# State-space batches of a two-layer encoder: the skip term as small TensorE products, five fixed PSUM banks, and separate buffers for outputs and in-chunk kernel

## The chip, the cores and the metric

The kernel runs on one core of a Trainium2 chip. A core has five engines that run side by side, each with its own in-order instruction queue: PE (TensorE, matrix products into PSUM), DVE (VectorE), ACT (ScalarE), POOL (GpSimd) and SP (SyncE, which here only issues DMAs). ACT issues a few DMAs as well. PSUM, where products land, has eight banks; each holds 128 partitions of 512 float32. The metric is the device time of one execution in microseconds; the median of several runs is compared.

## The reference

Input `x` is 1024 frames of 1024 channels in float32. Layer 0 projects the normalised input once; the projection feeds a state-space branch and a retention branch, each multiplied by its own SiLU gate, and one output projection follows. Layer 1 is a convolution module. Each layer adds to a residual, and a last RMS norm ends the work. Only the state-space branch matters here. In the reference, for each of 64 groups of 16 channels with 64 complex states:

```python
        bu_re = jnp.einsum('tbgh,gnh->tbgn', u_c, bb_re)
        bu_im = jnp.einsum('tbgh,gnh->tbgn', u_c, bb_im)
        pr, pim, zr, zi = lax.associative_scan(
            _complex_affine_combine, (a_r, a_i, bu_re, bu_im), axis=0)
        xr = zr + pr * s_re - pim * s_im
        xi = zi + pr * s_im + pim * s_re
        y = (jnp.einsum('tbgn,ghn->tbgh', xr, cre)
             - jnp.einsum('tbgn,ghn->tbgh', xi, cim)
             + dsk * u_c)
```

The term `dsk * u_c` is the skip: each channel's input times one number of that channel.

## The kernel before, in words

The front of layer 0 (`layer0_front`) makes the combined projection in blocks of 128 output columns. Blocks `u0` to `u7` are the inputs of the state-space branch; blocks `g8` to `g23` are the sixteen gate blocks. Each block is 2 halves of 512 frames times 8 row blocks times 3 products (float32 kept as a high and a low part: `xh`,`xl` and `wh`,`wl`), so 48 products of 512 columns on PE. DVE evacuates each half (line 393, times the norm factor R), ACT applies SiLU (394). The weight of a block is loaded by SP, its high part made on ACT (189) and its low part on DVE (190), two blocks ahead, in three rotating buffers.

Between the gate blocks lie eight state-space batches B = 0..7 of eight groups each. Time is cut into steps of 8 frames; within such a step a short convolution kernel acts, across steps a scan over 128 steps. A batch goes through four pieces:

- `s5_tables(B)`, one pair of gate blocks ahead: POOL makes the tables Mr, Mi, Tc, Ts and W3 (lines 766 to 768, 18 instructions); ACT makes R8 (839, four instructions, named R in the trace); for B > 1 DVE makes W2r and W2i from small tables that SP loads (806 to 811).
- `s5_states(B)`, traced at the start of gate block g(2B+8): PE makes V = W2 times U into two banks (868, 32 products); DVE turns V by Tc and Ts, scans it (883) and turns it back into S (876 to 895). PE makes the in-chunk kernel `kp` (902, 903), ACT copies columns 16 to 127 of it into `Kg` (905), and DVE writes columns 0 to 15 of `Kg` as the sum of `kp` and the skip table `dd` (906). PE transposes `Kg` into a second bank `kt` (908), ACT copies that (910), SP writes it to memory (912) and reads it back eightfold shifted as `Wd` (915), and ACT reorders `Wd` into W1 (917; the trace names W1 and W3 both W). `Wd` lies in the buffer of tag "yb".
- `s5_out(B)`, traced after gate block g(2B+10), one batch later: PE makes the output y from W1 and U (932) and from W3 and S (938) in two banks, ACT copies both into `yb` (942), which has the same single buffer as `Wd`, and stores it (944).

All these banks come from a pool of five (`ps_aux`) that hands out any free one; the gate blocks use three other banks. The order of the instructions on each engine is not written out by hand: a planner at build time simulates the program and puts every engine's instructions in an order by priority (the order in which they were traced, unless `at` sets it) and by its simulated time of readiness. `issue_after(x)` adds the rule that an instruction comes behind x on x's engine. On the chip every engine then follows that order, and waits in place for whatever is late. `retention` follows the front; it takes its banks from the same `ps_aux`.

## Time and profile before

| what | value |
|---|---|
| median of 3 runs | 1142.81 us (1140.18 to 1144.8) |
| the profiled execution | 1149.41 us, span 1147.6 us |
| mean granted PE clock | 0.993 |
| PE busy | 1125.1 us (98%) |
| DVE busy | 850.0 us (74%) |
| POOL busy | 654.7 us (57%) |
| ACT busy | 489.0 us (43%) |
| gate blocks and state-space batches | about 97 to 323 us of the span |

The profiled execution took 6.6 us longer than the median of the runs. Products on PE overlap, so a busy PE need not be at its peak; what counts is whether it waited, and at which clock it ran. A row of the timeline gives start, duration, engine, line, operation, the tiles as output<-inputs, shape and count, and in square brackets the engine's idle time before it with what ended it. A row of the waits gives the waiting instruction, what released it, the total, how often, and the longest. A row of the windows gives, for a stretch of the span, each engine's busy time and number of instructions, then the granted PE clock, the DMA share and GB/s.

### The profile page before, as it was taken

Reading aid. Unit: us, or ns where it says so; the run is one execution under the profiler, and the core shown is the slowest. Engines: PE = TensorE matmul, PEld = TensorE weight load, DVE = VectorE, ACT = ScalarE, POOL = GpSimd, SP = SyncE. Lnnn points to the kernel's source line nnn. Section 1 sums busy time; section 2 is a strip of 40 time slices with the busy share of each in tenths; the row PEclk is TensorE's granted clock in tenths of the full one; section 3 lists DMA queues with packets and bytes.
Section 4 is the critical chain, followed back from the end, with each engine's and each line's share of the span. In section 5 each row is a group of like instructions: output and inputs, shape, how many; then the busy total and the mean of one; then the engine's idle time right before and its main releaser. Section 6 shows DMA issues by size and latency. Waiting matters only on the chain.

```text
span 1147.6 us, 17204 instructions
## 1 busy us (share of the span) xinstructions
PE 1125.1 (98%) x6286; PEld 984.8 (86%) x6286; DVE 850.0 (74%) x1464; ACT 489.0 (43%) x719; POOL 654.7 (57%) x448
## 2 busy tenths in 40 slices
PE   9999989999999999999999999999999999999897
PEld 7888878888888888989887888888888888888787
DVE  6975778887417569486669522599999899999844
ACT  6423222232223231323436423545545676444673
POOL 2059999998236355232575111589544568677563
PEclk9999999999999999999999999999999999999999
DMA  9344345555378766859998988665778655367865
GB/s 353 110 135 153 120 151 175 194 186 179 133 259 278 265 215 193 284 185 333 386 361 299 318 297 283 189 234 203 250 246 297 239 178 172 121 195 250 273 229 191
DMA packets 117636, 261.45 MB, mean 228 GB/s; under 512 B 10672, under 2 KB 42288, under 8 KB 116912
## 3 DMA queue, kind: packets, MB, share of 16 engines
q1 hardware_dynamic: 114096, 247.78, 64.2%
q10 hardware_dynamic: 3456, 12.58, 2.9%
q8 instruction: 49, 0.80, 0.3%
q14 instruction: 35, 0.29, 0.1%
HBM read 181.48 MB, written 74.65 MB: 223 GB/s over the span
## 4 chain that ended last, share of the span: by engine, by line
PE 36%; DVE 8%; DMA 5%; POOL 2%; issue 2%; ACT 1%; POOLq 0%; SPq 0%; DVEq 0%; ACTq 0%
DVE cv L1534 6%; PE mm_wo L201 5%; PE mm_wo L200 5%; PE mm_wo L202 5%; PE mm_b L201 2%; PE mm_b L202 2%; PE mm_b L200 2%; PE mm_a L202 2%; PE mm_a L201 2%; PE mm_a L200 2%; PE mm_oc L202 2%; PE mm_oc L201 1%; PE mm_oc L200 1%; DMA yn<-yn_d 1%; DMA yg<-gs_d 1%
## 5 line engine op out<-in xcount | busy, mean ns | idle before, releaser
L1534 DVE SCALAR_TENSOR_TENSOR cv<-u,convw,cv 128x512 f32<-128x512 f32 x398 | 273.0, 749 | 6.7 <-ACT cv L1513 4.8
L1507 POOL TENSOR_TENSOR tp<-tp,tp 128x512 f32<-128x512 f32 x64 | 83.0, 1298 | 34.2 <-ACT tp L1506 33.2
L200 PE MATMUL mm_g<-xh,wh_g 128*128 128x512 f32 x256 | 99.6, 389 | 0.0
L201 PE MATMUL mm_g<-xl,wh_g 128*128 128x512 f32 x256 | 97.8, 382 | 0.0
L202 PE MATMUL mm_g<-xh,wl_g 128*128 128x512 f32 x256 | 97.7, 382 | 0.0
L437 POOL TENSOR_TENSOR s1q<-s1q,s1q 128x512 f32<-128x512 f32 x12 | 17.6, 1467 | 81.3 <-ACT s1q L432 81.3
L1506 ACT ACTIVATE tp<-u,convw 128x512 f32<-128x512 f32 x64 | 45.4, 718 | 36.1 <-POOL tp L1507 35.3
L200 PEld LDWEIGHTS mm_g<-xh,wh_g 128*128 128x128 f32 x256 | 48.9, 191 | 8.7 <-issue 1.2
L202 PEld LDWEIGHTS mm_g<-xh,wl_g 128*128 128x128 f32 x256 | 48.7, 190 | 7.1
L201 PEld LDWEIGHTS mm_g<-xl,wh_g 128*128 128x128 f32 x256 | 48.8, 191 | 6.9 <-issue 0.4
L190 POOL TENSOR_TENSOR wl_glu<-wf_glu,wh_glu 128x1024 fp32r<-128x1024 f32 x14 | 34.0, 2428 | 30.9 <-ACT wh_glu L189 30.9
L201 PE MATMUL mm_oc<-zl,wh_woc 128*128 128x512 f32 (+1 forms) x144 | 51.6, 359 | 0.0
L200 PE MATMUL mm_oc<-zh,wh_woc 128*128 128x512 f32 (+1 forms) x144 | 51.6, 370 | 0.0
L202 PE MATMUL mm_oc<-zh,wl_woc 128*128 128x512 f32 (+1 forms) x144 | 51.3, 359 | 0.2 <-DMA wl_woc<-lo_woc 0.2
L190 POOL TENSOR_TENSOR wl_v<-wf_v,wh_v 128x1024 fp32r<-128x1024 f32 x12 | 30.7, 2559 | 35.2 <-ACT wh_v L189 35.2
L393 DVE TENSOR_TENSOR gt<-mm_g,R 128x512 f32<-128x512 f32 x32 | 21.8, 682 | 38.6 <-PE mm_g L202 38.6
L201 PE MATMUL mm_u<-xl,wh_u 128*128 128x512 f32 x128 | 48.4, 381 | 0.7 <-DVE xl L316 0.7
L200 PE MATMUL mm_wo<-ysh,wh_wos 128*128 128x512 f32 x128 | 48.9, 382 | 0.0
L200 PE MATMUL mm_g<-h1h,wh_cg 128*128 128x512 f32 x128 | 48.9, 382 | 0.0
L201 PE MATMUL mm_b<-h1l,wh_cb 128*128 128x512 f32 x128 | 48.7, 381 | 0.1
L202 PE MATMUL mm_b<-h1h,wl_cb 128*128 128x512 f32 x128 | 48.6, 380 | 0.0
L201 PE MATMUL mm_wo<-ysl,wh_wos 128*128 128x512 f32 x128 | 48.5, 379 | 0.0
(526 smaller groups left out, 3641.5 us busy)
## 6 DMA issues: line engine op xcount, KB each, us to landing
wf_g<-w_ab SPq DMA_DIRECT2D x16, 512.0 KB
wf_wos<-w_out SPq DMA_DIRECT2D x16, 512.0 KB
wf_wor<-w_out SPq DMA_DIRECT2D x16, 512.0 KB
wf_cb<-w_c SPq DMA_DIRECT2D x16, 512.0 KB
wf_ca<-w_c SPq DMA_DIRECT2D x16, 512.0 KB
wf_woc<-w_out_c SPq DMA_DIRECT2D x16, 512.0 KB
wf_v<-w_v SPq DMA_DIRECT2D x12, 512.0 KB
wf_cg<-w_c SPq DMA_DIRECT2D x11, 512.0 KB
```

The source lines that it names most:

```text
L190: self.low_made = lo[i].tensor_tensor(wl[:].rearrange(fl)[:, c], wf[:, c], h.bitcast(F32), op=ALU.subtract)
L200: nc.tensor.matmul(ps, wh[:, kb, :], xh, start=start, stop=False, **more)
L201: nc.tensor.matmul(ps, wh[:, kb, :], xl, start=False, stop=False, **more)
L202: self.last_mm = nc.tensor.matmul(ps, wl[:, kb, :], xh, start=False, stop=stop, **more)
L393: nc.vector.tensor_tensor(nat(gt[:, c]), un(ps[:]), nat(self.R[:, c]), op=ALU.mult)
L437: nc.gpsimd.tensor_tensor(a, a, sq[:], op=ALU.add)
L1506: nc.scalar.mul(sk[:], u[:, k:k + HALF], cw[:, nb, k:k + 1])
L1507: gp.tensor_tensor(s0[:], s0[:], sk[:], op=ALU.add)
L1534: v.scalar_tensor_tensor(dst[:], *tap, accs_[i][:], op0=ALU.mult, op1=ALU.add)
```

## The change

1. The skip moves from DVE to PE. Between the two kinds of `kp` products PE now adds, per quarter, a product of a 32-column slice of the identity with the 16 columns of `dd`, into columns 0 to 15 of `kp`. The DVE sum is gone; `Kg` is one ACT copy of all 128 columns.
2. The banks of the batches are fixed: five tags y0, y1, v0, v1, kp with one bank each (`ps_s5`). `kt` is the second quarter of bank kp. The W2 of the first two batches, made by transposes, uses y0 and y1. The work before the batches and the retention each have a pool of five of their own.
3. `Wd` has a buffer of its own (4 KB a partition), no longer that of `yb`. The scratch that the program keeps for DMA descriptors is cut to 1024 bytes.
4. The W1 copy becomes `s5_local(B)`, traced after `s5_out(B-1)`, and comes behind the last `yb` copy of batch B-1 on ACT.
5. Two gates on DVE: the last two instructions of W2 (810, 811) come behind the evacuation of the first half of gate block g(2B+6), and the low part of the odd gate weights comes behind the last S instruction (895) of the batch that was traced last.

```diff
@@ wload_pieces
             nc.scalar.copy(h, wf[:, c])
-            self.low_made = lo[i].tensor_tensor(wl[:].rearrange(fl)[:, c], wf[:, c], h.bitcast(F32), op=ALU.subtract)
+            late = self.s5_end if name[0] == "g" and name[1:].isdigit() and int(name[1:]) % 2 and self.s5_end else None
+            with self.tc.issue_after(late.ins) if late else nullcontext():
+                self.low_made = lo[i].tensor_tensor(wl[:].rearrange(fl)[:, c], wf[:, c], h.bitcast(F32), op=ALU.subtract)
@@ run
             self.mid = self.pool("mid", 1, stack=mid)
-            self.ps_aux = self.pool("ps_aux", 5, PSUM, stack=mid)
             with ExitStack() as st:
                 self.layer0_front(st)
             with ExitStack() as st:
+                self.ps_aux = self.pool("ps_aux", 5, PSUM, stack=st)
                 self.retention(st)
@@ layer0_front
-        early = ExitStack()
+        early, aux = ExitStack(), ExitStack()
+        self.ps_aux = self.pool("ps_aux0", 5, PSUM, stack=aux)
...
         self.s5_turned()
+        aux.close()
+        self.ps_s5 = self.pool("ps_s5", 1, PSUM, stack=st)
         self.s5_tables(0)
...
-            if nb % 2 == 0 and B:
-                self.s5_out(B - 1)
+            if nb % 2 == 0:
+                if B:
+                    self.s5_out(B - 1)
+                self.s5_local(B)
@@ s5_w2
-        v.tensor_tensor(w2r[:], w2r[:], ptr[:], op=ALU.subtract)
-        v.tensor_tensor(w2i[:], w2i[:], pti[:], op=ALU.add)
+        with self.tc.issue_after(self.g_evac[2 * B + 6, 0].ins):
+            v.tensor_tensor(w2r[:], w2r[:], ptr[:], op=ALU.subtract)
+            v.tensor_tensor(w2i[:], w2i[:], pti[:], op=ALU.add)
@@ s5_states
-            ps = self.bank(f"w2{nm}_{B}")
+            ps = self.ps_s5.tile([P, HALF], F32, name=f"w2{nm}_{B}", tag=f"y{int(nm == 'i')}")
...
-            ps = self.bank(f"v{c}_{B}")
+            ps = self.s5_bank(f"v{c}", B)
...
-        v.tensor_tensor(c1(S[:, 1]), c0(zi), c0(t3), op=ALU.add)
+        self.s5_end = v.tensor_tensor(c1(S[:, 1]), c0(zi), c0(t3), op=ALU.add)
...
-        kp = self.bank(f"kp_{B}")
+        kp = self.s5_bank("kp", B)
         for q in range(4):
             o = kp[q * 32:(q + 1) * 32, :P]
             nc.tensor.matmul(o, self.cbr[:, q0 + q, :], Mr[:, q, :], start=True, stop=False)
+            nc.tensor.matmul(o[:, :16], self.ident[:, q * 32:(q + 1) * 32], self.dd[:, B, :], start=False, stop=False)
             nc.tensor.matmul(o, self.cbni[:, q0 + q, :], Mi[:, q, :], start=False, stop=True)
         Kg = w.tile([P, P], F32, name=f"Kg_{B}", tag="Kg", bufs=1)
-        nc.scalar.copy(Kg[:, 16:], kp[:, 16:P])
-        v.tensor_tensor(Kg[:, :16], kp[:, :16], self.dd[:, B, :], op=ALU.add)
-        kp = self.bank(f"kt_{B}")
-        nc.tensor.transpose(kp[:, :P], Kg[:], self.ident[:])
+        nc.scalar.copy(Kg[:], kp[:, :P])
+        nc.tensor.transpose(kp[:, P:2 * P], Kg[:], self.ident[:])
         Kt = w.tile([P, P], F32, name=f"Kt_{B}", tag="Kg", bufs=1)
-        nc.scalar.copy(Kt[:], kp[:, :P])
+        nc.scalar.copy(Kt[:], kp[:, P:2 * P])
...
-        Wd = w.tile([P, 8, P], F32, name=f"Wd_{B}", tag="yb", bufs=1)
+        Wd = w.tile([P, 8, P], F32, name=f"Wd_{B}", tag="Wd", bufs=1)
...
-        W1 = w.tile([P, 8, P], F32, name=f"W1_{B}", tag="W1", bufs=1)
-        nc.scalar.copy(W1[:].rearrange("p g (i h) -> p i g h", i=8), Wd[:].rearrange("p i (g h) -> p i g h", g=8))
-        self.s5_back[B] = U, W1, W3, S
+        self.s5_back[B] = U, Wd, W3, S
+
+    def s5_local(self, B):
+        U, Wd, W3, S = self.s5_back[B]
+        W1 = self.s5.tile([P, 8, P], F32, name=f"W1_{B}", tag="W1", bufs=1)
+        with self.tc.issue_after(self.yb_copy.ins) if B else nullcontext():
+            self.nc.scalar.copy(W1[:].rearrange("p g (i h) -> p i g h", i=8), Wd[:].rearrange("p i (g h) -> p i g h", g=8))
         self.s5_back[B] = U, W1, W3, S
@@ s5_out
-        ps = [self.bank(f"y{g2}_{B}") for g2 in range(2)]
+        ps = [self.s5_bank(f"y{g2}", B) for g2 in range(2)]
...
-            nc.scalar.copy(yb[:].rearrange("p (q g) m -> p q g m", g=2)[:, :, g2, :],
+            self.yb_copy = nc.scalar.copy(yb[:].rearrange("p (q g) m -> p q g m", g=2)[:, :, g2, :],
```

More of the change, by code (lines that the diff above doesn't have):

```diff
@@ L127, in plan @@
         self.wseq, self.wissued, self.wgot = seq, {}, 0
-        self.low_load, self.early_low = {}, None
+        self.low_load, self.early_low, self.s5_end = {}, None, None
         self.wnames, self.lo_d = {n for _, n in seq}, {}
@@ L366, in scaled @@
                 cb(h, ps)
-        self.u_evac = {}
+        self.u_evac, self.g_evac = {}, {}
         def u_block(nb):
@@ L392, in evac @@
                 c = slice(h * HALF, (h + 1) * HALF)
-                nc.vector.tensor_tensor(nat(gt[:, c]), un(ps[:]), nat(self.R[:, c]), op=ALU.mult)
+                self.g_evac[nb, h] = nc.vector.tensor_tensor(nat(gt[:, c]), un(ps[:]), nat(self.R[:, c]), op=ALU.mult)
                 nc.scalar.activation(gt[:, c], gt[:, c], AF.Silu)
@@ L768, in outer, with s5_bank @@
             yield gp.tensor_tensor(o, o, t[:], op=op)
+    def s5_bank(self, tag, B):
+        return self.ps_s5.tile([P, HALF], F32, name=f"{tag}_{B}", tag=tag)
     def s5_turned(self):
@@ L1919 @@
     arrays = layout(inputs)
-    nc = bacc.Bacc("TRN2", target_bir_lowering=False, num_devices=1)
+    nc = bacc.Bacc("TRN2", target_bir_lowering=False, num_devices=1, dynamic_dma_scratch_size=1024)
     A = {k: nc.dram_tensor(k, v.shape, F32, kind="ExternalInput").ap() for k, v in arrays.items()}
```

## The prediction

> **What bounds the kernel now.** I read the page's busy times first, then who PE waited for, then the windows, then the timeline around the one place that the change touches.

> ```profile
> span 1147.6 us, 17204 instructions
> PE 1125.1 (98%) x6286; PEld 984.8 (86%) x6286; DVE 850.0 (74%) x1464; ACT 489.0 (43%) x719; POOL 654.7 (57%) x448
> ```

> ```profile
> PE kt L908 <- DVE Kg L906: 3.3, 1, 3.3
> PE cst L509 <- DVE cs L1616: 2.9, 1, 2.9
> PE ro L1221 <- DVE sc L1198: 2.6, 1, 2.6
> PE mm_glu L200 <- DVE mm_gluz L1397: 2.6, 1, 2.6
> PE idle L292 <- DVE mhalf L237: 1.1, 1, 1.1
> ```

> PE is busy nearly throughout, and only four of its waits are longer than 1.1 us. So an edit shows in the time if it adds to PE's queue or if it touches one of these waits. Exactly one of them lies in the batches: the transpose of `Kg`, once, for 3.3 us. The windows show that the batches are otherwise limited by PE alone:

> ```profile
> 158.66:162.31 3.65, 0.38 (x2) 0.00 (x0) 3.65 (x7) 0.00 (x0) 3.57 (x4) 0.97 0.25 99
> 162.31:166.00 3.69, 3.69 (x11) 3.03 (x12) 3.69 (x5) 0.00 (x0) 3.61 (x4) 0.57 0.00 0
> 181.50:208.98 27.48, 27.48 (x195) 23.98 (x193) 23.74 (x28) 8.22 (x15) 26.93 (x20) 1.00 0.51 175
> 208.98:236.46 27.48, 27.48 (x195) 23.98 (x193) 23.05 (x28) 8.22 (x15) 25.95 (x19) 1.00 0.52 179
> ```

> Columns: PE, weight loads, DVE, ACT, POOL, clock, DMA. From 181.5 us on, a batch takes 27.48 us, all of it PE time, with POOL at 25.95 to 26.93 close behind. In the first row PE stands still; in the second the clock is 0.57 for 3.7 us. The timeline of PE shows both costs:

> ```profile
> 151.65 0.48 PE L200 MATMUL mm_g<-xh,wh_g 128*128 128x512 f32 x1
> ...
> 158.66 0.38 PE L202 MATMUL mm_g<-xh,wl_g 128*128 128x512 f32 x1
> 162.31 0.47 PE L908 MATMUL kt<-ident,Kg 128*128 128x128 f32 x1 [3.27 <-DVE Kg L906]
> 162.44 0.77 PE L200 MATMUL mm_g<-xh,wh_g 128*128 128x512 f32 x1
> 163.00 0.63 PE L201 MATMUL mm_g<-xl,wh_g 128*128 128x512 f32 x1
> 163.43 0.63 PE L202 MATMUL mm_g<-xh,wl_g 128*128 128x512 f32 x1
> ...
> 165.53 0.38 PE L201 MATMUL mm_g<-xl,wh_g 128*128 128x512 f32 x1
> 165.75 0.38 PE L202 MATMUL mm_g<-xh,wl_g 128*128 128x512 f32 x1
> ```

> A gate product normally starts 0.22 us after the one before (165.53 to 165.75); here the next start comes 162.31 - 158.66 = 3.65 us later, a loss of 3.43. Behind it the spacing is 0.43 (163.00 to 163.43) for about eight products, so 8 x 0.21 = 1.7 us more. The place costs 5.1 us.

> Why was `Kg` late? ACT and DVE, read backwards:

> ```profile
> 138.38 0.24 ACT L910 COPY Kt<-kt 128x128 f32<-128x128 f32 x1
> ...
> 150.75 1.05 ACT L917 COPY W<-Wd 128x1024 f32<-128x1024 f32 x1 [10.23 <-DMA Wd<-k_d]
> ...
> 153.36 1.05 ACT L189 CAST wh_g<-wf_g 128x1024 fp32r<-128x1024 f32 x1
> ...
> 155.39 0.25 ACT L905 COPY Kg<-kp 128x112 f32<-128x112 f32 x1 [0.45 <-DMA PTi<-pt_d]
> ```

> ```profile
> 154.44 2.13 DVE L190 TENSOR_TENSOR wl_g<-wf_g,wh_g 128x1024 fp32r<-128x1024 f32 x1 [4.48 <-ACT wh_g L189]
> ...
> 160.58 1.60 DVE L807 TENSOR_TENSOR W2i<-PTr,BTi 128x512 f32<-128x512 f32 x1
> 162.10 0.16 DVE L906 TENSOR_TENSOR Kg<-kp,s_s_dd 128x16 f32<-128x16 f32 x1
> ```

> ACT had its part of `Kg` at 155.64, three microseconds before PE reached the transpose. The 0.16 us sum on DVE stood last in a queue that began late, at 154.44, because ACT had stood 10.23 us at the W1 copy of batch 1 for `Wd`, with the weight cast behind it. `Wd` in turn was late since `Kt` was copied only at 138.38.

> **The change, part by part.**

> *The sum off DVE.* DVE loses 8 x 0.16 = 1.3 us, none of it on the path. `Kg` is then one ACT copy, of 128 columns instead of 112, which costs nothing that PE sees. At the stall, ACT's copy ended 2.9 us ahead of PE's arrival even in this late batch, so if PE's order stays the wait goes: -3.43 us, and with it the half clock, -1.70. What is late next there: V's own users on DVE, whose banks PE needs again only at 181.68 (below), 19 us on.

> The half clock deserves a check. All four windows with a long PE wait have a clock below 1.00 (this one above, and):

> ```profile
> 480.00:520.00 40.00, 37.41 (x279) 34.03 (x278) 29.66 (x82) 11.03 (x13) 15.31 (x9) 0.96 0.64 210
> ...
> 600.00:640.00 40.00, 37.45 (x166) 31.97 (x165) 38.32 (x52) 26.39 (x42) 17.27 (x10) 0.96 0.86 290
> ...
> 1040.00:1080.00 40.00, 37.07 (x160) 30.59 (x159) 37.34 (x57) 20.90 (x30) 30.40 (x18) 0.96 0.82 273
> ```

> So waits of 2.6 to 3.3 us were followed by half clock here, and I count the 1.70 in full. [...]

> *The new products.* Eight batches times four products of 32 weight columns and 16 data columns. The nearest rows are the `kp` products, of the same weights and 128 data columns:

> ```profile
> 103.92 0.45 PE L902 MATMUL kp<-Mr,s_s_cbr 128*32 128x128 f32 x8
> 104.17 0.42 PE L903 MATMUL kp<-Mi,s_s_cbi 128*32 128x128 f32 x8
> 104.52 0.48 PE L201 MATMUL mm_g<-xl,wh_g 128*128 128x512 f32 x1
> ```

> Four products, recorded as eight, take 0.25 us of PE's queue (103.92 to 104.17), or 0.35 where a switch to other work is included. Were only the data columns to count, it would be 16/128 of 0.25, 0.03. I take 0.25, since the weights are loaded all the same: 8 x 0.25 = +2.0 us, between +0.2 and +2.8. All of it is on the path, because PE has no idle time there. This is sure to be paid; the gain hangs on a single wait.

> *Fixed banks; kt in the bank of kp.* `kt` waits for `Kg` anyway, which has read kp by then. V of the next batch needs banks v0 and v1, so S must be done with them:

> ```profile
> 146.40 0.67 DVE L895 TENSOR_TENSOR S<-v,d 128x508 f32<-128x508 f32 x1
> ...
> 149.16 1.09 PE L868 MATMUL v<-U,W2r 128*64 128x128 f32 x16
> ...
> 174.51 1.70 DVE L190 TENSOR_TENSOR wl_g<-wf_g,wh_g 128x1024 fp32r<-128x1024 f32 x1
> ...
> 176.73 0.67 DVE L895 TENSOR_TENSOR S<-v,d 128x508 f32<-128x508 f32 x1
> ...
> 181.68 1.09 PE L868 MATMUL v<-U,W2r 128*64 128x128 f32 x16
> ```

> The last reader of the banks (895) ends at 147.1, 2.1 us ahead of the next V in the tightest batch, and at 177.4, 4.3 us ahead, one batch later. Cost 0; if the cover went, PE would wait for the difference. The two y banks are free after the `yb` copies, a batch ahead. Bounds: 0, and one new wait of 3.4 + 1.7 us.

> *`Wd` and `yb` apart, W1 behind yb.* `Wd` no longer waits for the store of the y before, and the y copies no longer wait for W1. With `Kg` early, `Kt` and `Wd` come earlier too, and much of ACT's 10.23 us should vanish. PE waited for none of it except through the stall, so its own worth is 0. In the other direction, W1 stays in ACT's queue with the SiLU, the weight casts and the next `Kg` behind it; ACT standing there costs PE nothing until a cast or `Kg` is late.

> *The gates.* The low part of an odd weight comes behind S instead of before it (174.51 and 176.73): S is done 1.6 us sooner, the weight 1.3 us later, for a block that starts after the rest of the current one and the next, each 48 x 0.22 = 10.3 us. W2's last two instructions come behind a gate evacuation, and hold up DVE's queue until PE has made that half block; behind them would be the rest of the turn and S. The tightest case is batch 2:

> ```profile
> 144.12 1.76 DVE L811 TENSOR_TENSOR W2i<-W2i,PTi 128x512 f32<-128x512 f32 x1
> ```

> It ends at 145.9, 3.3 us before its V at 149.16, and that batch's gate (the evacuation of g10) lies earlier. I take 0; the bounds are -1 (S earlier helps nobody on PE, so no more than the small waits it might remove) and again one wait of 5.1.

> *Addresses, the descriptor scratch and the planner.* The tiles move in SBUF, so the first loads of the retention may wait for other tiles, and the planner may order later work otherwise. After the batches PE has at least the first k and q blocks (2 x 10.3 us) ahead of it before it needs the retention's transposes, which covers a few microseconds. I take 0 and price it in the rivals.

> *Sum.* On the profiled execution, 1149.41 (its span 1147.6 and 1.8 around it): -3.43 - 1.70 + 2.0 = -3.1, so 1146.3. That execution stands 6.6 above the median, so the forecast for the median is 1142.81 - 3.1 = 1139.7.

> **The rivals.**

> *The wait moves, or is the profile's own.* The stall was born of one late DMA in an execution 6.6 us slower than the median; undisturbed it may be short, or PE may wait at the next thing in that batch. Then only the products count: 1142.8 + 2.0 = 1144.8. For it: all later batches pass the same transpose without a wait. Against: the planned order gives DVE the same queue each time.

> *Slower: `Kg` waits in ACT's queue.* Now PE reaches the transpose 7 us after kp (151.65 to 158.66 in batch 2) because the planner expects DVE. With the short ACT copy it may place the transpose right behind. ACT had `Kg` at 155.64, 4.0 us after 151.65. From the point where the planned distance falls under ACT's real delay, PE stands. ACT's waits are long:

> ```profile
> ACT R L839 <- DVE v L883: 50.8, 7, 11.4
> ...
> ACT W L917 <- DMA Wd<-k_d: 15.3, 2, 10.2
> ```

> One such wait costs what is won (1144.8); two, at 5.1 each, give 1139.7 + 10.3 = 1150.0. Against: in the steady batches `Kg` stands ahead of R in ACT's queue, and `Wd` should be early.

> *Faster: a later wait goes as well.* The three other long waits hang on DVE being late by 2.6 to 2.9 us; with the half clock each is worth some 4.3. A shifted order could remove one (1135.4) or two (1131). It could add one as easily, but the three are there to be lost.

> *It does nothing.* No wait changes and the products hide: 1142.8. PE has no idle time to hide them, so I fold this into the first rival.

> **How the numbers follow.** Forecast (wait and half clock go) 0.42, its own range 1136.5 to 1143; wait moves 0.20; slower by ACT's queue 0.17; a later wait goes 0.21. The predicted time is 1139.7. To leave out two tenths, the range runs from two later waits gone (1131) to two new ones (1150). A change of 0.5%, 5.7 us, is about what a measurement of this kernel can tell from none: below 1137.1 lie the later wait gone and a tail of the forecast, 0.21 + 0.10 = 0.31; above 1148.5 the slower rival and a little more, 0.20; between them 0.49.

> **What the changed profile would show.** Right: no wait of PE for `Kg` or anything else between 97 and 323 us, clock 1.00 throughout there, no DVE row on `Kg`; a new row of eight recorded products between the two of `kp`, adding about 0.25 us, and a steady batch of 27.7 instead of 27.48; batch 2 without its 5 us; ACT's wait for `Wd` well under 10 us. Wrong, if PE waits for `Kg` from ACT or for V's banks, if the steady batch grows by more than 0.4 us, if the batches end less than 2 us sooner, or if the gain is there at 323 us and lost to a new wait in the retention or behind it.

## The result, and the profile after

The changed kernel takes 1148.92 us (median of 22 runs, 1144.74 to 1151.44), the kernel before 1144.83 (22 runs, 1140.18 to 1150.02; the three runs shown ahead of the prediction had a median of 1142.81). The ratio is 1.0029, 95% interval 1.0016 to 1.0043: about 3.3 us slower (the medians stand 4.1 apart), where I had forecast 3.1 us faster. The profiled execution took 1150.49 us, 1.6 over the median.

The page and the waits of PE, of the changed kernel:

```profile
span 1148.7 us, 17305 instructions
...
PE 1129.4 (98%) x6350; PEld 992.1 (86%) x6350; DVE 846.3 (74%) x1456; ACT 489.3 (43%) x719; POOL 655.4 (57%) x448
```

```profile
PE cst L516 <- DVE cs L1632: 2.8, 1, 2.8
PE ro L1237 <- DVE sc L1214: 2.0, 1, 2.0
PE mm_glu L202 <- DVE mm_gluz L1413: 2.0, 1, 2.0
PE mm_oc L204 <- DMA wl_woc<-lo_woc: 1.5, 1, 1.5
```

The wait for `Kg` is gone, and no other has come up in the batches. PE has 64 records more: 8 batches of four new products, each recorded as two passes. The gain was made, then. The loss stands in the steady batches (windows; PE, weight loads, DVE, ACT, POOL, clock, DMA):

```profile
181.00:209.26 28.26, 28.26 (x204) 24.80 (x202) 22.53 (x28) 8.18 (x15) 27.71 (x20) 1.00 0.52 171
209.25:237.51 28.26, 28.26 (x203) 24.79 (x202) 23.11 (x28) 8.23 (x15) 27.19 (x20) 1.00 0.54 170
```

A batch takes 28.26 us where it took 27.48, still without any wait of PE. So 8 x 0.78 = 6.2 us more work is in PE's queue, not 2.0. The timeline of PE shows where:

```profile
209.25 0.41 PE L913 MATMUL kp<-Mr,s_s_cbr 128*32 128x128 f32 x2
209.50 0.18 PE L914 MATMUL kp<-s_s_dd,ident 128*32 128x16 f32 x1
209.50 0.30 PE L913 MATMUL kp<-Mr,s_s_cbr 128*32 128x128 f32 x1
209.53 0.18 PE L914 MATMUL kp<-s_s_dd,ident 128*32 128x16 f32 x1
209.56 0.28 PE L915 MATMUL kp<-Mi,s_s_cbi 128*32 128x128 f32 x1
209.64 0.27 PE L913 MATMUL kp<-Mr,s_s_cbr 128*32 128x128 f32 x1
209.67 0.27 PE L915 MATMUL kp<-Mi,s_s_cbi 128*32 128x128 f32 x1
209.75 0.18 PE L914 MATMUL kp<-s_s_dd,ident 128*32 128x16 f32 x1
209.75 0.30 PE L913 MATMUL kp<-Mr,s_s_cbr 128*32 128x128 f32 x1
...
210.30 0.39 PE L915 MATMUL kp<-Mi,s_s_cbi 128*32 128x128 f32 x2
210.62 0.48 PE L202 MATMUL mm_g<-xh,wh_g 128*128 128x512 f32 x1
```

The group of in-chunk kernel products takes 1.37 us (209.25 to 210.62). Before it took 0.60, with all eight Mr records starting within 0.25 us and all eight Mi records behind them: the four quarters of the array, to which the products of 32 columns go, worked side by side. Now the quarters start one after the other, 0.25 us apart (209.25, 209.50, 209.75). The new products are short, 0.18 us each; what they cost is the overlap of the others.

In the two profiled executions, the stretch from the products named `turn` to the first product of k is 227.89 us before and 229.66 after. The sum there is 6.2 more for the products and 5.1 less for the wait and its half clock, 1.1; the other 0.7 was not traced to a cause. From there to the end it is 824.7 and 824.5 us: nothing behind the batches changed by much, and PE's products stand there in the old order.

### The profile page after: what moved, and what is told of

Its sections match the earlier page's. It is cut to its first block, busy times and chain, and to the rows that moved or that the text cites. A ratio compares the mean times of both kernels' runs of the same rounds, so it can differ in the third digit from the quotient of the medians.

```text
span 1148.7 us, 17305 instructions
## 1 busy us (share of the span) xinstructions
PE 1129.4 (98%) x6350; PEld 992.1 (86%) x6350; DVE 846.3 (74%) x1456; ACT 489.3 (43%) x719; POOL 655.4 (57%) x448
## 4 chain that ended last, share of the span: by engine, by line
PE 30%; DVE 16%; DMA 3%; issue 2%; POOL 2%; ACT 2%; SPq 0%; POOLq 0%; DVEq 0%; ACTq 0%
DVE cv L1550 12%; PE mm_wo L204 5%; PE mm_wo L203 5%; PE mm_wo L202 5%; PE mm_oc L204 2%; PE mm_glu L202 1%; PE mm_glu L204 1%; PE mm_oc L203 1%; PE mm_glu L203 1%; PE mm_oc L202 1%; PE mm_b L204 1%; PE mm_a L204 1%; PE mm_a L202 1%; PE mm_b L202 1%; PE mm_b L203 1%
## 5 line engine op out<-in xcount | busy, mean ns | idle before, releaser
L202 PE MATMUL mm_g<-xh,wh_g 128*128 128x512 f32 x256 | 98.9, 386 | 0.0
L202 PEld LDWEIGHTS mm_g<-xh,wh_g 128*128 128x128 f32 x256 | 48.6, 190 | 8.6 <-PE kp L913 1.0
L202 PE MATMUL mm_oc<-zh,wh_woc 128*128 128x512 f32 (+1 forms) x144 | 51.5, 369 | 0.0
L202 PE MATMUL mm_wo<-ysh,wh_wos 128*128 128x512 f32 x128 | 49.0, 383 | 0.0
L202 PE MATMUL mm_g<-h1h,wh_cg 128*128 128x512 f32 x128 | 49.0, 383 | 0.0
L203 PE MATMUL mm_a<-h1l,wh_ca 128*128 128x512 f32 x128 | 48.6, 380 | 0.0
```

The lines of the kernel that those rows point to most:

```text
L202: nc.tensor.matmul(ps, wh[:, kb, :], xh, start=start, stop=False, **more)
L203: nc.tensor.matmul(ps, wh[:, kb, :], xl, start=False, stop=False, **more)
```

## The experiments

Each was compared with the kernel before on its own chip. There the kernel before had a median of 1143.96 us (e1 to e4), 1144.75 (e5 and e6) and 1144.89 (e9 to e11), so kernels of different chips are compared by their ratios and not by their medians. The batch length is that of the steady batches in the profile, and the last column is when PE first works on k, the end of the batches.

| kernel | ratio to before, 95% interval | median us | kp group us | batch us | batches end at us |
|---|---|---|---|---|---|
| before | | 1144.83 | 0.60 | 27.48 | 322.9 |
| before, profiled once more (e9) | 0.9992 [0.9975, 1.0010] | 1144.55 | | 27.49 | 319.4 |
| the change | 1.0029 [1.0016, 1.0043] | 1148.92 | 1.37 | 28.26 | 324.1 |
| e1: by kind | 0.9967 [0.9952, 0.9982] | 1140.45 | 0.63 | 27.53 | 318.0 |
| e2: sum on DVE | 0.9977 [0.9962, 0.9992] | 1140.95 | 0.59 | 27.49 | 317.8 |
| e3: products alone | 1.0029 [1.0008, 1.0049] | 1147.19 | | 28.26 | 324.1 |
| e4: one wide product | 0.9991 [0.9973, 1.0009] | 1142.61 | 0.84 | 27.71 | 319.6 |
| e5: pairs | 0.9971 [0.9956, 0.9987] | 1142.10 | 0.65 | 27.55 | 318.2 |
| e6: by kind, alone | 0.9982 [0.9965, 0.9999] | 1143.78 | 0.64 | 27.53 | 317.7 |
| e10: e1 again | 0.9975 [0.9956, 0.9994] | 1143.18 | | 27.53 | 318.2 |
| e11: e6 again | 0.9963 [0.9944, 0.9983] | 1141.69 | | 27.53 | 317.9 |

**e1, the order of the products.** The theory is that the loss is the order: quarter by quarter, three products each. The edit puts the twelve products in order by kind, and `chained` keeps the planner from changing that order:

```diff
-        for q in range(4):
-            o = kp[q * 32:(q + 1) * 32, :P]
-            nc.tensor.matmul(o, self.cbr[:, q0 + q, :], Mr[:, q, :], start=True, stop=False)
-            nc.tensor.matmul(o[:, :16], self.ident[:, q * 32:(q + 1) * 32], self.dd[:, B, :], start=False, stop=False)
-            nc.tensor.matmul(o, self.cbni[:, q0 + q, :], Mi[:, q, :], start=False, stop=True)
+        o = [kp[q * 32:(q + 1) * 32, :P] for q in range(4)]
+
+        def by_kind():
+            for q in range(4):
+                yield nc.tensor.matmul(o[q], self.cbr[:, q0 + q, :], Mr[:, q, :], start=True, stop=False)
+            for q in range(4):
+                yield nc.tensor.matmul(o[q][:, :16], self.ident[:, q * 32:(q + 1) * 32], self.dd[:, B, :], start=False, stop=False)
+            for q in range(4):
+                yield nc.tensor.matmul(o[q], self.cbni[:, q0 + q, :], Mi[:, q, :], start=False, stop=True)
+        self.chained(by_kind())
```

> The changed kernel with the twelve in-chunk kernel products of a batch issued by kind: four of Mr, four of the skip, four of Mi, so that neighbours always go to different quarters of the array. Theory (order): the quarters then run side by side as they did before, the group takes 0.6 + 0.25 = 0.85 us instead of 1.36, a steady batch 27.7 us instead of 28.26, the whole 8 x 0.5 = 4 us less than the change, about 1144.8 (ratio 1.000 to before). Rival (a product of 16 columns costs its 0.19 us wherever it stands): group 1.36, time 1148.9, ratio 1.0035.

```profile
206.03 0.43 PE L915 MATMUL kp<-Mr,s_s_cbr 128*32 128x128 f32 x8
206.27 0.23 PE L917 MATMUL kp<-s_s_dd,ident 128*32 128x16 f32 x8
206.33 0.40 PE L919 MATMUL kp<-Mi,s_s_cbi 128*32 128x128 f32 x8
206.66 0.48 PE L202 MATMUL mm_g<-xh,wh_g 128*128 128x512 f32 x1
```

The timeline of PE shows the quarters side by side again. All eight passes of the skip take 0.06 us (206.27 to 206.33), and the batch is 27.53 us. The four added products cost 0.05 us a batch in this order and 0.78 in the other. The time fell further than I expected, to a ratio of 0.9967 and not 1.000. I had allowed 0.2 us a batch more than was needed, which is about 1.6 of these 3.8 us; the rest was not explained, and is smaller in e10, the same kernel again (0.9975).

**e2, the products taken out.** The skip is summed on DVE as before, and the rest of the change stays:

```diff
-            nc.tensor.matmul(o[:, :16], self.ident[:, q * 32:(q + 1) * 32], self.dd[:, B, :], start=False, stop=False)
...
-        nc.scalar.copy(Kg[:], kp[:, :P])
+        nc.scalar.copy(Kg[:, 16:], kp[:, 16:P])
+        v.tensor_tensor(Kg[:, :16], kp[:, :16], self.dd[:, B, :], op=ALU.add)
```

> The changed kernel with the skip added by VectorE again (as before) and no products for it; banks, buffers and gates stay as in the change. Theory (the loss is the products alone): a steady batch is 27.48 us again and the time falls by 8 x 0.78 = 6.2 us to about 1142.7, ratio 0.998, if the transpose of Kg no longer waits; if its wait for VectorE comes back, 3.4 to 5.1 us of that are lost again: 1146 to 1147.8, ratio 1.001 to 1.003. Rival (banks, buffers or gates cost the rest): no wait at Kg and still not under 1145.

```profile
PE ro L1237 <- DVE sc L1214: 3.0, 1, 3.0
PE cst L516 <- DVE cs L1632: 3.0, 1, 3.0
PE mm_glu L202 <- DVE mm_gluz L1413: 2.2, 1, 2.2
PE idle L295 <- DVE mhalf L239: 1.1, 1, 1.1
```

The waits of PE in this kernel have none for `Kg`, although DVE again stands between kp and the transpose. The timelines of DVE and of PE, in the batch that had stalled:

```profile
156.90 0.16 DVE L917 TENSOR_TENSOR Kg<-kp,s_s_dd 128x16 f32<-128x16 f32 x1
158.85 0.27 PE L918 MATMUL kp<-ident,Kg 128*128 128x128 f32 x1
```

The sum ends at 157.06, 1.8 us before PE comes to the transpose. So the rest of the change takes the wait away without the products, in this one profile; which of banks, buffers and gates does it was not tested. The batch is 27.49 us, the batches end 6.3 us before those of the change (317.8 against 324.1), and the ratio of 0.998 is the one expected.

**e3, the products alone.** The kernel before with the new products in the order of the change, and nothing else of it (the diff is the two hunks of e2 the other way round).

> The kernel before with the skip moved to TensorE as in the change and nothing else of it. Theory: the wait at Kg goes (3.4 us, 5.1 with the half clock) and the products cost 6.2: 1146 to 1147.6, ratio 1.001 to 1.0025, a steady batch 28.26 us. Rival (the wait went because of the separate buffers, which let ScalarE be early): the wait stays, at about 3 us and on ScalarE, and the time is 1151, ratio 1.0054.

```profile
207.28:235.54 28.26, 28.26 (x202) 24.77 (x201) 23.99 (x27) 8.34 (x16) 27.71 (x21) 1.00 0.53 174
```

A batch takes 28.26 us, there is no wait for `Kg`, and the ratio is 1.0029, that of the whole change. The products alone make the loss, and they too remove the wait. The change held two cures for one wait, and only the products cost anything that shows.

**e4, one product for all quarters.** One product over 128 partitions behind the eight others:

```diff
-            nc.tensor.matmul(o[:, :16], self.ident[:, q * 32:(q + 1) * 32], self.dd[:, B, :], start=False, stop=False)
             nc.tensor.matmul(o, self.cbni[:, q0 + q, :], Mi[:, q, :], start=False, stop=True)
+        nc.tensor.matmul(kp[:, :16], self.ident[:], self.dd[:, B, :], start=False, stop=True, skip_group_check=True)
```

> The changed kernel with the skip as one product over all 128 partitions and 16 columns behind the eight others, in place of four over 32 partitions. Theory (order): the eight others run side by side again and the wide one adds about 0.25 us: a steady batch 27.7 us, time about 1144.8, ratio 1.000. Rival (fixed price per product of 0.19): 27.48 + 0.2, nearly the same, so this run tells only whether one wide product is the cheap form; anything over 28 us a batch would speak against both.

```profile
206.90 0.45 PE L913 MATMUL kp<-Mr,s_s_cbr 128*32 128x128 f32 x8
207.14 0.42 PE L914 MATMUL kp<-Mi,s_s_cbi 128*32 128x128 f32 x8
207.50 0.40 PE L915 MATMUL kp<-s_s_dd,ident 128*128 128x16 f32 x2
207.74 0.46 PE L202 MATMUL mm_g<-xh,wh_g 128*128 128x512 f32 x1
```

It covers all 128 columns of the array, and the next gate product starts 0.24 us behind it (207.50 to 207.74). This is about the price that I had given the four small ones, and with it the kernel ties with before (0.9991).

**e5, pairs.** What in the order breaks the overlap? In the rows of the change above quarter 0 has six passes, two for each product, and quarter 1's first pass starts with quarter 0's third (209.50 and 209.50), when three of quarter 0's are still to come. My estimate from these starts is that four passes of a quarter are taken up at a time, one in work and three waiting, and that a fifth holds up everything behind it in program order, that of quarter 1 included. Before, a quarter had four passes in a row, and the group took 0.60 us. In e5 each quarter gets a product of Mr and one of the skip, four passes in a row, and the Mi products come behind:

```diff
             for q in range(4):
                 yield nc.tensor.matmul(o[q], self.cbr[:, q0 + q, :], Mr[:, q, :], start=True, stop=False)
-            for q in range(4):
                 yield nc.tensor.matmul(o[q][:, :16], self.ident[:, q * 32:(q + 1) * 32], self.dd[:, B, :], start=False, stop=False)
```

(Against e1.)

> The changed kernel with the products in pairs: per quarter one of Mr and one of the skip, quarter after quarter, and the four of Mi behind them. Theory (each quarter of the array takes one pass in work and three waiting, and what comes behind them for any quarter is held back): a pair is four passes, so the quarters still run side by side; the group takes about 0.65 us, a steady batch 27.5 to 27.6 us, the time is that of the order by kind, ratio 0.997. Rival (a short product between two long ones of its quarter is what breaks the overlap): the group is over 1 us, a batch about 28, ratio 1.001 or more.

```profile
206.16 0.45 PE L915 MATMUL kp<-Mr,s_s_cbr 128*32 128x128 f32 x8
206.40 0.24 PE L916 MATMUL kp<-s_s_dd,ident 128*32 128x16 f32 x7
206.46 0.28 PE L918 MATMUL kp<-Mi,s_s_cbi 128*32 128x128 f32 x1
206.47 0.18 PE L916 MATMUL kp<-s_s_dd,ident 128*32 128x16 f32 x1
206.47 0.41 PE L918 MATMUL kp<-Mi,s_s_cbi 128*32 128x128 f32 x7
206.81 0.48 PE L202 MATMUL mm_g<-xh,wh_g 128*128 128x512 f32 x1
```

The program says Mr, skip, Mr, skip; PE worked on all the Mr first, then on the skips. The group takes 0.65 us and the batch 27.55, as that estimate has it. A short product between two others does no harm here.

**e7 and e8, a full-width product instead.** The kernel of e2 with one more product per quarter that adds nothing, an identity slice by 128 columns of zeros; in e7 quarter by quarter, in e8 by kind:

```diff
+        self.zp = sp.tile([P, P], F32, name="s5_zp")
+        v.memset(self.zp[:], 0.0)
...
             nc.tensor.matmul(o, self.cbr[:, q0 + q, :], Mr[:, q, :], start=True, stop=False)
+            nc.tensor.matmul(o, self.ident[:, q * 32:(q + 1) * 32], self.zp[:], start=False, stop=False)
             nc.tensor.matmul(o, self.cbni[:, q0 + q, :], Mi[:, q, :], start=False, stop=True)
```

> The changed kernel with the skip summed on VectorE (a steady batch 27.49 us), and between the two in-chunk kernel products of each quarter one more of the same size, identity slice by zeros, 128 columns, which adds nothing. Theory (six passes in a row for one quarter block the queue, however long they are): the group of 24 passes takes 1.4 to 1.6 us, a batch 28.3 to 28.5. Rival (the 16 columns are at fault): the full-width product overlaps as the other two do, group 0.85, batch 27.75.

> The same product by zeros of 128 columns, but ordered by kind: four of Mr, four by zeros, four of Mi. Theory: they run side by side and add what the rows of the two others showed, 0.22 to 0.25 us: group 0.83, batch 27.7 to 27.75. Rival (the array takes no third kind at full overlap): group above 1 us.

The timelines of PE, first e7:

```profile
210.06 0.41 PE L915 MATMUL kp<-Mr,s_s_cbr 128*32 128x128 f32 x2
210.30 0.27 PE L916 MATMUL kp<-s_zp,ident 128*32 128x128 f32 x1
210.30 0.30 PE L915 MATMUL kp<-Mr,s_s_cbr 128*32 128x128 f32 x1
...
210.55 0.27 PE L916 MATMUL kp<-s_zp,ident 128*32 128x128 f32 x1
210.55 0.30 PE L915 MATMUL kp<-Mr,s_s_cbr 128*32 128x128 f32 x1
...
211.57 0.48 PE L202 MATMUL mm_g<-xh,wh_g 128*128 128x512 f32 x1
```

and e8:

```profile
206.45 0.43 PE L917 MATMUL kp<-Mr,s_s_cbr 128*32 128x128 f32 x8
206.69 0.40 PE L919 MATMUL kp<-s_zp,ident 128*32 128x128 f32 x8
206.91 0.40 PE L921 MATMUL kp<-Mi,s_s_cbi 128*32 128x128 f32 x8
207.24 0.48 PE L202 MATMUL mm_g<-xh,wh_g 128*128 128x512 f32 x1
```

Quarter by quarter, the full-width product blocks exactly as the short one did: the next quarter starts with the third pass of the one before (210.30, 210.55), the group takes 1.51 us and the batch 28.41. By kind it adds 0.22 us, and the batch is 27.69. So in these runs the number of passes in a row for one quarter, six in e7 and two in e8, decided whether the quarters overlapped, and not their width, and 0.25 us would have been a fair price for products of 128 columns in the right order. Each of the two kernels had one execution, 1147.0 and 1145.1 us.

**e9, the kernel before once more.** In the trace of before, the half clock stands in stretches of 3.413 us (162.08 to 165.49 at 0.50, then 1.00 again). The four ahead of the end begin at 162.08, 493.17, 609.23 and 1076.85 us, which is 97, 34 and 137 times 3.413 apart.

> The kernel before, unchanged, to see what its wait at Kg is worth in other executions than the one profiled. Theory (the wait recurs, since the order on every engine is fixed, but half clock follows it only where the wait falls right on the clock's own grid of 3.41 us): the profile shows a wait of PE for Kg of about 3 us again, the executions' clocks spread from about 0.993 to 0.999, one halved stretch being 0.0015 of the clock and 1.7 us, and the times follow the clocks. Rival (the wait was an accident of the one execution): no wait over 1 us at Kg.

Its timeline of PE, its timeline of ACT, and its windows at the wait:

```profile
158.91 0.38 PE L202 MATMUL mm_g<-xh,wl_g 128*128 128x512 f32 x1
160.41 0.33 PE L908 MATMUL kt<-ident,Kg 128*128 128x128 f32 x1 [1.12 <-DVE Kg L906]
```

```profile
149.44 1.05 ACT L917 COPY W<-Wd 128x1024 f32<-128x1024 f32 x1 [8.56 <-DMA Wd<-k_d]
```

```profile
160.41:164.00 3.59, 3.59 (x18) 3.19 (x19) 3.59 (x4) 0.00 (x0) 3.51 (x3) 1.00 0.00 0
```

The wait is there again, but it is 1.12 us and not about 3 as I had expected, with the clock at 1.00 behind it. ACT waited 8.56 us for `Wd` instead of 10.23. So the place cost 1.3 us in this execution (160.41 - 158.91 - 0.22) and 5.1 in the other. Two profiles don't give the mean, but with 6.2 us for the products they give a loss of 1.1 to 4.9, and the measured 3.3 lies between.

**e6, e10 and e11: the products by kind, with and without the rest.** e6 and e11 are one kernel, the kernel before with nothing but the products in the order of e1; e10 is e1 again on the same chip as e11.

> The kernel before with nothing but the skip on TensorE, its products ordered by kind. Theory (the products' order is the loss and the wait at Kg the gain, and banks, buffers and gates are worth nothing beside that): no wait at Kg, a steady batch 27.53 us, ratio 0.996 to 0.998, as with the whole change in that order. Rival (separate buffers and gates carry part of the gain): it stays a microsecond or more behind the whole change in that order, 0.998 or above, with a wait in the batches.

> The changed kernel with the products by kind, on the same chip as the next one. Theory (the other parts of the change are worth nothing once the wait at Kg is gone): the same time as the next within 1 us. Rival (they carry some of the gain): 1.5 us or more below the next, as the two differed on two chips (0.9967 and 0.9982).

> The kernel before with the skip on TensorE by kind and nothing else, beside the one before it. Theory: the same time within 1 us, ratio 0.997 to before. Rival: 1.5 us or more above it, with the difference in waits for DMAs behind the batches.

e6 had stood 1.5 thousandths behind e1, on another chip, and had 2.3 us of wait for a weight's low part near the end. On one chip, e11 is 1.5 us ahead of e10 (1141.69 and 1143.18, with overlapping intervals). I had expected them within 1 us; the rival, e11 behind e10, did not hold. The batches end at 317.7 to 318.2 us in all four profiles of the two kernels. Fixed banks, separate buffers and gates are worth nothing that shows once the skip is on PE in the right order. Both kernels beat the kernel before by 2 to 4 us in each of their two measurements, and so beat the change.

## Why the prediction was wrong

*What bounds the kernel* was right: PE's queue and a few waits. In all thirteen profiles, the stretch from the `turn` products to the first product of k is that of e2 (223.15 us, no wait and no new product), plus eight times what a batch grew over e2's, plus the cost of the wait for `Kg` (5.1 us, and 1.3 in e9), to within 0.4 us.

*The sum off DVE* was right in kind: the wait went, and nothing took its place. Its size, 5.1 us, was that of one execution. I had noted that it was 6.6 us slower than the median and named as a rival that the wait might be shorter elsewhere, but I took the full 5.1 for the forecast. e9 measured 1.3.

*The new products* is the step that failed. I gave them 2.0 us, between 0.2 and 2.8; they cost 6.2. Two of the signs that I had named for being wrong came with it: the steady batch grew by 0.78 us, more than 0.4, and in the profiled execution the batches ended 1.3 us later (324.15 against 322.89) and not 2 us sooner. That the measured time lies within the stated range all the same is luck, since the range was drawn for waits that go or come. I took the price from rows in which all Mr products stand together and all Mi products behind them, and I priced a third kind as one more such row. But the program issues them quarter by quarter, Mr and Mi in turn. The grouped rows were the outcome of an overlap in the array, and the change broke it. The row gave the price of a product beside others, not of a product that pushes the others apart. In the order by kind the products cost 0.05 us a batch, in the order of the change 0.78; my bounds for a batch, 0.03 to 0.35, held the first and not the second.

*The slower rival*, `Kg` held up in ACT's queue, did not come. ACT in the changed kernel:

```profile
145.28 1.08 ACT L958 COPY yb<-y 128x512 f32<-128x512 f32 x2 [0.40 <-ACT gt L397]
146.24 1.07 ACT L933 COPY W<-Wd 128x1024 f32<-128x1024 f32 x1
...
154.21 0.27 ACT L917 COPY Kg<-kp 128x128 f32<-128x128 f32 x1 [1.90 <-PE kp L915]
```

The W1 copy found `Wd` ready, and `Kg` was copied as soon as kp was done. That half of the reasoning held: with `Kt` early (129.99 in place of 138.62), the 10.23 us of ACT vanished. In e3, without the new buffers, `Kt` was done at 135.53 and ACT did not wait for `Wd` either. The kernel lost on the side for which I had named no rival, PE's own queue.

*Banks, buffers, gates* at 0 held beside the products (e10 and e11), and so did the guess that work behind the batches would not move. e2 showed what I had not seen: banks, buffers and gates remove the wait without the products. (48 x 0.22 us is 10.6 and not the 10.3 written there; nothing rests on it.)

*The half clock* was counted in full because every long wait of that profile showed it. That was four cases of one execution. In e1 the wait of 2.7 us near 1063 us brought none:

```profile
1040.00:1080.00 40.00, 37.19 (x168) 31.18 (x167) 35.78 (x55) 24.22 (x33) 27.26 (x17) 1.00 0.79 266
```

where the same place before had 0.96. In the trace of the change three halved stretches ahead of the end, of 3.413 us each at a clock of 0.50, begin at 492.60, 608.65 and 1076.28 us, and as in before (e9) 34 and 137 times 3.413 apart. A wait need not be that long: the four long waits of PE in before were 2.6 to 3.3 us. A difference shows when each profile is divided into stretches of 3.413 us, counted from the start of one of its halved ones. In before, the five stretches in which PE stood idle longest, 1.94 to 3.28 us in sum (the ends of products are modelled), were each followed by a halved one, and the next, with 0.99 us, was not; in the change four with 1.79 to 2.37 us were, and the next, with 1.53 us, was not. Over the thirteen profiles, all 39 stretches with 1.79 us or more were followed by a halved one; of those with 1.74 us or less, only one of 1.65 us in e4 was. (In e5 and e10 one halving lasted a second stretch, although PE idled for less; that stays open.) The wait of 3.27 us in before had 3.04 us within one stretch, from 158.67 to 162.08. The one of 2.74 us in e1 was divided, 1.50 and 1.24 us, and the one of 1.12 us in e9 is shorter than all of these. So the waits of 2.0 to 3.4 us here were followed by a halved stretch, worth 1.7 us behind the wait for `Kg` in before, or by none, by where they fell. Over the 22 executions of the change the mean clock ran from 0.992, at 1151.44 us, to 1.000, at 1145.65; the slower executions mostly have the lower clock (correlation -0.75).

What stays open: e1's median lies 8.5 us below that of the change, but the two were taken on different chips. By the ratios to the kernel before, the distance is 0.0062, 7.1 us, and 0.0054, 6.2 us, with e10. The products explain 8 x 0.73 = 5.8. That leaves 0.4 to 1.3 us, which the intervals of the ratios (0.0013 to 0.0019 to either side) can't tell from nothing. The change's profile also has three halved stretches ahead of the end and e1's one, and 1.5 us of wait for a weight's low part against 0.7; whether that comes with the shifted position of all later work was not settled. Which part of banks, buffers and gates takes the wait away, and how many passes of a quarter are taken up at a time, were not settled either.

## What to carry to other kernels

A price taken from a merged row of small TensorE products is that of their overlap: before adding a product to such a group, look at how many passes in a row go to one part of the array in program order, and issue products for different parts in turn. Here the same four added products cost 0.05 or 0.78 us a batch by order alone. And a wait that occurs once in a profile should be priced by more than one execution, the half clock behind it as a chance: here it stood behind a wait of 3.27 us in before, and not behind 2.74 us in e1 or 1.12 us in e9.
